# An mLSTM layer whose heads' scores and sums are regrouped on TensorE, with two later issues

## The chip, the cores and the metric

The kernel runs on one core of a Trainium2 chip. Five engines work beside each other: TensorE (PE in the profile; its weight loads are PEld) multiplies matrices into the eight banks of PSUM, VectorE (DVE) and ScalarE (ACT) do elementwise work, GpSimd (POOL) and SyncE (SP) mostly issue transfers here. The metric is the device time of one execution, in microseconds (us). The time before is the median of three runs, 894.86 us (893.63 to 895.79).

## The reference

One decoder layer on 512 tokens of width 1024. A normalised input is multiplied by a wide matrix and feeds two branches: an mLSTM with four heads and a sliding-window attention. Both are merged with sigmoid gates, projected and added to the input; a squared-ReLU MLP and a gated embedding follow, and a last normalisation. The part that matters here, in formulas for one mLSTM head (the kernel takes all 512 tokens as one chunk):

```python
scores = einsum("thk,shk->ts", q, k) * exp(log_d - m_t)   # causal
num = scores @ v ;  den = scores.sum(-1)
h = num / maximum(abs(den), exp(-m_t))
h = h * rsqrt(mean(h * h) + EPS) * norm_g * sigmoid(o)    # y_a
merged = sigmoid(g_a) * (y_a @ w_branch_a) + sigmoid(g_b) * (y_b @ w_branch_b)
x = x + merged @ w_out
...
out = x * rsqrt(mean(x * x) + EPS) * g_fin                # the last norm
```

## The kernel before

All activations stay on the chip; weights stream in as 512 KB transfers on SP's queue. Almost every product has both operands split into a high and a low part (`split`, L133 to L141: ScalarE casts the high part at L137, VectorE subtracts at L138) and is made of three TensorE products (high-high, high-low, low-high) of 512 columns at L171. Weights go through four buffers each of high and low parts (wh, wl), so a weight's cast waits until the product four weights earlier is done with its buffer. The products of the output projection and of the MLP's second half are in a form with seven products of blocks instead of eight, with sums of blocks as operands: `merge_sums` (L887) makes the activations' sums.

PSUM is shared by tags. In the first pool psg has two tiles of one bank, pst two of one bank, psa two of two banks. A tile taken when all are in use waits until one is released. For the output projection the pool is closed and another opened, with three pairs of two banks (psp) and two banks psg at the start of the memory.

The order of the instructions is not the program's. A planner simulates the program and lists, engine by engine, what to issue next among the instructions that it takes to be ready, the earlier in the program first. Each engine then works its list strictly in order, and waits on a semaphore where a real predecessor is late. `tc.keep_in_program_order(ins)` pins an instruction behind the one traced before it on its engine. `with tc.issue_after(ins):` keeps what is traced in the block behind `ins`, but only on the engine of `ins`: instructions of the block that run on another engine are not held.

The mLSTM stage (L767 to L864): `ml_weights(h)` computes a head's decays by ten exponentials on ScalarE (L788), its scores in four products with plain f32 operands into pst banks (L795; each appears as two TensorE instructions), and multiplies both on VectorE (L796). `ml_out(h)` sums the values with these weights, for each of four blocks of 128 tokens in a pst bank (L805, one to four products of 257 columns, the last column being the denominator), copies the result to SBUF on ScalarE (L808) and the denominator on VectorE (L809), and squares it for the norm (L817). `ml_norm` scales the heads (L829), with the output gate fetched back from DRAM. `branch_b(i)` is one of eight products with w_branch_b (24 TensorE products into a psg bank, evicted by VectorE at L838), `ya_of(h)` transposes a head's result (L847). The heads' loop mixes these: two branch products and one head per turn, and the transposes two heads behind.

Then `merge(i)` for i from 0 to 7 multiplies with w_branch_a into psg and evicts at L873 and L874, `merge_sums` follows each second one, and `out_proj` begins: the first product of F11 into X (two psg banks), copied out to q1 by ScalarE (L992) and added to the residual by transfers from GpSimd's queue (L995), then F12 accumulated onto the same X.

At the end of the kernel, `columns_of` (L944) transposes the residual for the last gated product, a psp tile for each column set, evicted by L140 on ScalarE and L141 on VectorE, and `ple` (L1198 evicts) makes the embedding's product. The final gain g_fin is loaded at L1188 and scaled into two versions by L1191 and L1192 on VectorE; it is used in the last norm (L1265, L1281).

`stir` (L259) issues small products into an idle psg tile at the start, to keep TensorE busy.

Of the kernel before, what the change touches and what calls it, by code (L numbers as in the profile page):

```python
# [36 lines left out]
def block_kernel(  # L37
# [221 lines left out]
    idle = ps_g()  # L259

    def stir(n):
        for i in range(n):
            tc.keep_in_program_order(T.matmul(idle[:, :P], ones, ones, start=True, stop=True))
# [8 lines left out]
    for i in range(2):  # L272
        for c in range(2):
            tc.keep_in_program_order(
                T.matmul(gmix[:, c * 512 : (c + 1) * 512], one_row, gparts[c][i], start=i == 0, stop=i == 1, skip_group_check=True)
            )
        stir(1 if i == 0 else 3)
# [495 lines left out]
    def ml_weights(h):  # L773
# [9 lines left out]
        for s in range(NT):  # L783
            dm = act_f("dm")
            n0 = s * P
# [8 lines left out]
            psc = ps_t()  # L794
            T.matmul(psc[:, n0:], qk[4 + h][:, n0 : n0 + P], qk[h][:, n0:], start=True, stop=True)  # L795
            V.tensor_mul(dm[:, n0:], psc[:, n0:], dm[:, n0:])  # L796
            wT.append(dm)
        wts[h] = wT

    def ml_out(h):  # L800
        wT = wts.pop(h)
        for t in range(NT):
            pn = ps_t()
            for s in range(t + 1):
                T.matmul(  # L805
                    pn[:, : DV + 1], wT[s][:, t * P : (t + 1) * P], vm[s][:, h, :], start=s == 0, stop=s == t
                )
            A.copy(h_of(h, t), pn[:, :DV])  # L808
            V.tensor_copy(hd[:, h, t : t + 1], pn[:, DV : DV + 1])  # L809
# [40 lines left out]
    ml_weights(0)  # L850
    rds = []
    for h in range(NH):
        branch_b(2 * h)
        if h + 1 < NH:
            ml_weights(h + 1)
        rds.append(ml_out(h))
        branch_b(2 * h + 1)
        if h == 1:
            ml_norm([0, 1], rds)
        elif h > 1:  # L860
            ml_norm([h], rds[h:])
            ya_of(h - 2)
    ya_of(2)
    ya_of(3)  # L864
# [22 lines left out]
    def merge_sums(even, odd):  # L887
# [8 lines left out]
        for two, src in (((G1, G2), sa), ((G3, G4), sb)):  # L896
            hl = act_hl("ms")
            split(hl, src)
            for n in range(2):
                two[n].append([q[:, n * 256 : (n + 1) * 256] for q in hl])  # L900

# [12 lines left out]
    for j in range(4):  # L914
# [10 lines left out]
        merge_sums(m0, merge(2 * j + 1))  # L925
# [35 lines left out]
    def out_proj():  # L961
# [29 lines left out]
        for t in range(2):  # L991
            A.copy(q1[t], X[t])  # L992
# [198 lines left out]
    V.tensor_scalar_mul(glast, gfin, D**0.5 / 8192)  # L1191
    V.tensor_scalar_mul(gfin, gfin, -(D**0.5) / 8192)  # L1192
# [17 lines left out]
    with tc.issue_after(evicted):  # L1210
        for m in range(NT):
# [181 lines left out]
```

## Time and profile before

| | |
|---|---|
| median of three runs | 894.86 us (893.63 to 895.79) |
| the profiled execution | 894.56 us |
| its span, first to last instruction | 892.8 us |
| granted TensorE clock | 0.999 |
| instructions | 11819 |
| data moved by DMA | 105.19 MB, mean 118 GB/s |

A row of a timeline has the start in us from the span's start, the length in us, the engine, the line of the kernel and the operation, then the tile written and those read ("psg<-ya,wh"), the shapes, and the number of instructions merged into the row. A bracket at its end is the time that the engine stood idle before it, and what ended the wait. TensorE's products overlap in the rows (one starts while the last still drains), so a row's length is more than a product's share of the time. A row by line gives instead the shortest, median and longest duration in ns, the first and last start, and the forms.

### The profile page before, as it was taken

How to read it: one execution, taken by the hardware profiler on the slowest of the kernel's cores; microseconds unless marked ns; L12 is line 12 of the kernel's file. 1: busy time of each engine (PE TensorE's matmuls, PEld its weight loads, DVE VectorE, ACT ScalarE, POOL GpSimd, SP SyncE). 2: the span in 40 equal slices, each digit the busy share in tenths (PEclk: the TensorE clock that was granted, in tenths of full speed). 3: DMA queues.
4: the chain of work that ended last, by engine and by line, in shares of the span. 5: the costliest groups of instructions: out<-in, count | busy, mean ns of one | idle time of the engine just before them, and what ended most of it. 6: DMA issues, size and time to landing. Idle time of an engine off the chain costs nothing.

```text
span 892.8 us, 11819 instructions
## 1 busy us (share of the span) xinstructions
PE 876.9 (98%) x4452; PEld 731.2 (82%) x4452; DVE 665.0 (74%) x1074; ACT 488.6 (55%) x810; POOL 30.3 (3%) x53
## 2 busy tenths in 40 slices
PE   8999999999999999999989999999999999999996
PEld 7888889998877677788878888888888888888786
DVE  6899787874887967557896669746966784699566
ACT  6684554454775767654343566345435534544753
POOL 2111010000000000000020000000000000000000
PEclk9999999999999999999999999999999999999999
DMA  7775254434212162346234711630352054102402
GB/s 273 195 184 177 71 173 162 163 118 165 72 48 72 29 206 74 116 123 240 89 52 136 258 49 39 206 108 25 112 177 88 1 189 142 48 24 61 152 1 95
DMA packets 32363, 105.19 MB, mean 118 GB/s; under 512 B 4525, under 2 KB 5037, under 8 KB 32306
## 3 DMA queue, kind: packets, MB, share of 16 engines
q1 hardware_dynamic: 28002, 93.15, 31.3%
q0 software_dynamic: 4160, 11.02, 4.7%
q8 instruction: 35, 0.57, 0.3%
q10 hardware_dynamic: 144, 0.26, 0.1%
q14 instruction: 22, 0.18, 0.1%
HBM read 91.30 MB, written 8.40 MB: 112 GB/s over the span
## 4 chain that ended last, share of the span: by engine, by line
PE 93%; DMA 2%; DVE 2%; ACT 1%; issue 0%; SPq 0%; DVEq 0%; ACTq 0%
PE psg L171 52%; PE psp L171 23%; PE psa L171 7%; PE pst L171 4%; PE pst L805 2%; PE pst L734 1%; PE psa L726 1%; PE pst L795 1%; PE psa L689 1%; PE psa L690 1%; DMA wr<-in_w_vsif 1%; DMA gfin<-in_g_fin 1%; DMA wr<-in_w_gb 0%; PE pst L847 0%; DVE wl L138 0%
## 5 line engine op out<-in xcount | busy, mean ns | idle before, releaser
L138 DVE TENSOR_TENSOR wl<-wr,wh 128x1024 fp32r<-128x1024 f32 x138 | 167.6, 1220 | 91.7 <-ACT wh L137 91.3
L137 ACT CAST wh<-wr 128x1024 fp32r<-128x1024 f32 x138 | 144.7, 1050 | 163.0 <-PE psg L171 60.8
L171 PE MATMUL psg<-x,wh 128*128 128x512 f32 x512 | 157.7, 389 | 0.0
L171 PE MATMUL psp<-wh,uf 128*128 128x512 f32 x448 | 139.1, 389 | 0.0
L171 PEld LDWEIGHTS psg<-x,wh 128*128 128x128 f32 x512 | 96.0, 188 | 19.9
L171 PE MATMUL psg<-x,wl 128*128 128x512 f32 x256 | 99.6, 389 | 0.0
L171 PEld LDWEIGHTS psp<-wh,uf 128*128 128x128 f32 x448 | 84.1, 188 | 17.3
L171 PE MATMUL psp<-wl,uf 128*128 128x512 f32 x224 | 87.3, 390 | 0.0
L171 PE MATMUL psg<-h,wh 128*128 128x512 f32 x256 | 81.4, 396 | 0.0
L137 ACT CAST wh<-wd 128x1024 fp32r<-128x1024 f32 x44 | 46.3, 1053 | 57.1 <-PE psp L171 23.1
L138 DVE TENSOR_TENSOR wl<-wd,wh 128x1024 fp32r<-128x1024 f32 x44 | 53.3, 1220 | 15.5 <-ACT wh L137 15.4
L171 PEld LDWEIGHTS psg<-h,wh 128*128 128x128 f32 x256 | 46.9, 188 | 13.5 <-issue 4.9
L171 PEld LDWEIGHTS psg<-x,wl 128*128 128x128 f32 x256 | 48.1, 188 | 9.9
L171 PE MATMUL psg<-h,wl 128*128 128x512 f32 x128 | 50.3, 393 | 0.0
L138 DVE TENSOR_TENSOR uf<-F,uf 128x1792 fp32r<-128x1792 f32 (+2 forms) x20 | 33.0, 1652 | 22.1 <-ACT uf L137 22.1
L171 PEld LDWEIGHTS psp<-wl,uf 128*128 128x128 f32 x224 | 42.1, 188 | 8.7
L171 PE MATMUL psg<-yb,wh 128*128 128x512 f32 x128 | 43.2, 411 | 0.0
L171 PE MATMUL psg<-ya,wh 128*128 128x512 f32 x128 | 40.1, 393 | 0.0
L137 ACT CAST uf<-F 128x1792 fp32r<-128x1792 f32 (+2 forms) x20 | 27.9, 1395 | 20.8 <-DVE F L1095 20.7
L1119 DVE SCALAR_TENSOR_TENSOR xk<-psp,r,xk 128x512 f32<-128x512 f32 x48 | 33.9, 746 | 3.5 <-PE psp L171 3.2
L171 PE MATMUL psg<-hS,wh 128*128 128x256 f32 x192 | 35.6, 284 | 0.0
L171 PE MATMUL psa<-h,wh 128*128 128x256 f32 x192 | 35.3, 285 | 0.3 <-ACT p L625 0.3
(313 smaller groups left out, 1782.3 us busy)
## 6 DMA issues: line engine op xcount, KB each, us to landing
wr<-in_w_up SPq DMA_DIRECT2D x32, 512.0 KB, 3.3
wd<-in_w_down SPq DMA_DIRECT2D x24, 512.0 KB, 3.7
wr<-in_w_qsw SPq DMA_DIRECT2D x8, 512.0 KB, 4.1
gd<-gr POOLq DMA_DIRECT2D x8, 512.0 KB, 3.3
wr<-in_w_qkml SPq DMA_DIRECT2D x8, 512.0 KB, 3.4
wr<-in_w_b SPq DMA_DIRECT2D x8, 512.0 KB, 3.3
gl<-gd SPq DMA_DIRECT2D x8, 512.0 KB, 3.3
wr<-in_w_a SPq DMA_DIRECT2D x8, 512.0 KB, 3.8
```

The lines of the kernel that those rows point to most:

```text
L137: A.copy(dst[0], src)
L138: last_low[0] = V.tensor_sub(dst[1], src, r32(dst[0]))
L171: last_mm[0] = T.matmul(ps, l, r, start=first and i == 0, stop=last and i == len(ops) - 1, skip_group_check=parts)
L689: T.matmul(o, q[:, n * P : (n + 1) * P], kk[kp][ab][:, k0 : k0 + 256], start=True, stop=False)
L690: T.matmul(o, q[:, n * P : (n + 1) * P], kl[kp][ab][:, k0 : k0 + 256], start=False, stop=True)
L726: T.transpose(pt[:, c : c + P], lm3[ab][:, g, j * P : (j + 1) * P], ident)
L734: T.matmul(o[HALF[ab], :], vs[n + 1 - nk + j][:, c : c + 64], pTs[j][:, ab * 512 : (ab + 1) * 512], start=j == 0, stop=j == nk - 1,)
L795: T.matmul(psc[:, n0:], qk[4 + h][:, n0 : n0 + P], qk[h][:, n0:], start=True, stop=True)
L805: T.matmul(pn[:, : DV + 1], wT[s][:, t * P : (t + 1) * P], vm[s][:, h, :], start=s == 0, stop=s == t)
L1119: pin(V.scalar_tensor_tensor(o, ps[:, t, :], r2[:, 2 * toks + t : 2 * toks + t + 1], o, ALU.mult, ALU.add))
```

## The change

Four things change. (1) A head's decays (`ml_decay`) are separated from its scores (`ml_scores`). The scores go into one psa tile of two banks and one pst bank, the score for s=3 sharing a bank with that for s=1; the sums go two token blocks at a time into the two banks of a psa tile and are evicted together, the later half first. A head's sums are kept behind its branch product, and the next head's scores behind these sums. One branch product is left in each turn of the loop; the other four come after it, each followed by the transposes of one head. (2) The idle tile at the start becomes two. (3) The second half of the last `merge_sums` is returned as a function and called after the copies to q1. (4) The two scalings of g_fin move into the block after the last copy of the embedding's product.

```diff
-    idle = ps_g()
+    idle = [ps_g(), ps_g()]
-    def stir(n):
+    def stir(n, bank=0):
         for i in range(n):
-            tc.keep_in_program_order(T.matmul(idle[:, :P], ones, ones, start=True, stop=True))
+            tc.keep_in_program_order(T.matmul(idle[bank][:, :P], ones, ones, start=True, stop=True))
...
-        stir(1 if i == 0 else 3)
+        stir(1 if i == 0 else 3, i)
...
-    def ml_weights(h):
+    def ml_decay(h):
...
-            psc = ps_t()
-            T.matmul(psc[:, n0:], qk[4 + h][:, n0 : n0 + P], qk[h][:, n0:], start=True, stop=True)
-            V.tensor_mul(dm[:, n0:], psc[:, n0:], dm[:, n0:])
...
+    def ml_scores(h):
+        two, one = ps_a(), ps_t()
+        banks = [two[:, :512], two[:, 512:], one, two[:, 512:]]
+        at = [0, 0, 0, 384]
+        for s in (0, 1, 3, 2):
+            n0 = s * P
+            psc = banks[s][:, at[s] : at[s] + S - n0]
+            T.matmul(psc, qk[4 + h][:, n0 : n0 + P], qk[h][:, n0:], start=True, stop=True, skip_group_check=True)
+        for s in range(NT):
+            n0 = s * P
+            dm = wts[h][s]
+            V.tensor_mul(dm[:, n0:], banks[s][:, at[s] : at[s] + S - n0], dm[:, n0:])
...
     def ml_out(h):
         wT = wts.pop(h)
-        for t in range(NT):
-            pn = ps_t()
-            for s in range(t + 1):
-                T.matmul(
-                    pn[:, : DV + 1], wT[s][:, t * P : (t + 1) * P], vm[s][:, h, :], start=s == 0, stop=s == t
-                )
-            A.copy(h_of(h, t), pn[:, :DV])
-            V.tensor_copy(hd[:, h, t : t + 1], pn[:, DV : DV + 1])
+        for half in (1, 0):
+            pn = ps_a().rearrange("p (n c) -> p n c", n=2)
+            for t in (2 * half, 2 * half + 1):
+                for s in range(t + 1):
+                    last_mm[0] = T.matmul(
+                        pn[:, t % 2, : DV + 1], wT[s][:, t * P : (t + 1) * P], vm[s][:, h, :], start=s == 0, stop=s == t, skip_group_check=True
+                    )
+            A.copy(hs[h][half].rearrange("p (n c) -> p n c", n=2), pn[:, :, :DV])
+            V.tensor_copy(hd[:, h, 2 * half : 2 * half + 2], pn[:, :, DV])
...
-    ml_weights(0)
+    ml_decay(0)
+    ml_scores(0)
     rds = []
     for h in range(NH):
-        branch_b(2 * h)
+        branch_b(h)
         if h + 1 < NH:
-            ml_weights(h + 1)
-        rds.append(ml_out(h))
-        branch_b(2 * h + 1)
+            ml_decay(h + 1)
+        with tc.issue_after(last_mm[0].ins):
+            rds.append(ml_out(h))
+        if h + 1 < NH:
+            with tc.issue_after(last_mm[0].ins):
+                ml_scores(h + 1)
         if h == 1:
             ml_norm([0, 1], rds)
         elif h > 1:
             ml_norm([h], rds[h:])
-            ya_of(h - 2)
-    ya_of(2)
-    ya_of(3)
+    for h in range(NH):
+        branch_b(NH + h)
+        ya_of(h)
...
-        for two, src in (((G1, G2), sa), ((G3, G4), sb)):
+
+        def parts(two, src):
             hl = act_hl("ms")
             split(hl, src)
...
+        parts((G1, G2), sa)
+        return lambda: parts((G3, G4), sb)
...
-        merge_sums(m0, merge(2 * j + 1))
+        later = merge_sums(m0, merge(2 * j + 1))
+        if j < 3:
+            later()
...
-            A.copy(q1[t], X[t])
+            copied = A.copy(q1[t], X[t])
+        with tc.issue_after(copied.ins):
+            later()
...
-    V.tensor_scalar_mul(glast, gfin, D**0.5 / 8192)
-    V.tensor_scalar_mul(gfin, gfin, -(D**0.5) / 8192)
...
     with tc.issue_after(evicted):
+        V.tensor_scalar_mul(glast, gfin, D**0.5 / 8192)
+        V.tensor_scalar_mul(gfin, gfin, -(D**0.5) / 8192)
```

More of the change, by code (lines that the diff above doesn't have):

```diff
@@ L784, in ml_weights @@
             dm = act_f("dm")
-            n0 = s * P
             for t in range(s, NT):
```

## The prediction

> **What bounds the kernel now.** I read the page's busy table first, then a table of stretches, then the chain of waits, then the timelines of TensorE (PE), ScalarE (ACT) and VectorE (DVE) around each place that the diff touches.
>
> ```profile
> PE 876.9 (98%) x4452; PEld 731.2 (82%) x4452; DVE 665.0 (74%) x1074; ACT 488.6 (55%) x810; POOL 30.3 (3%) x53
> PE 93%; DMA 2%; DVE 2%; ACT 1%; issue 0%; SPq 0%; DVEq 0%; ACTq 0%
> 338.80:414.00 75.20, 75.20 (x336) 58.86 (x336) 44.58 (x101) 47.52 (x115) 0.00 (x0) 1.00 0.41 139
> 452.40:461.10 8.70, 6.21 (x26) 4.88 (x27) 8.66 (x14) 5.95 (x9) 0.01 (x1) 1.00 0.00 0
> 824.80:840.80 16.00, 14.60 (x80) 11.99 (x79) 10.69 (x15) 10.64 (x17) 0.00 (x0) 1.00 0.58 195
> ```
>
> TensorE is busy for 98% of the span and makes up 93% of the chain that ended last. A change can therefore shorten the kernel only where TensorE stands still or loses time between products. The three stretches are the ones that the diff touches; after the length and a comma, their columns are busy time and count of PE, PEld, DVE, ACT and POOL, then TensorE's granted clock. In the mLSTM stretch (338.8 to 414) TensorE is covered for all 75.20 us, so nothing like an idle gap can be won there. At the start of the output projection (452.4 to 461.1) it stands still for 2.5 us of 8.7, and at the last norm's columns for 1.4 us of 16. The clock is full in all three.
>
> ```profile
> 443.40 0.61 PE L171 MATMUL psg<-ya,wh 128*128 128x512 f32 x2
> 443.85 0.39 PE L171 MATMUL psg<-ya,wl 128*128 128x512 f32 x1
> 444.08 0.61 PE L171 MATMUL psg<-ya,wh 128*128 128x512 f32 x2
> 453.27 0.47 PE L171 MATMUL psg<-wh,mg 128*128 128x512 f32 x1 [0.88 <-DVE sga L873]
> 460.60 0.50 PE L171 MATMUL psg<-wh,mg 128*128 128x512 f32 x1 [1.62 <-ACT q L992]
> 824.81 1.04 PE L944 MATMUL psp<-ident,xk 128*128 128x128 f32 x8
> 831.66 0.60 PE L944 MATMUL psp<-ident,xk 128*128 128x128 f32 x4
> 833.05 0.66 PE L944 MATMUL psp<-ident,xk 128*128 128x128 f32 x4 [0.79 <-DVE x L141]
> 834.31 0.66 PE L944 MATMUL psp<-ident,xk 128*128 128x128 f32 x4 [0.61 <-DVE x L141]
> ```
>
> The first three rows give the pitch: three products of 512 columns between 443.40 and 444.08, so 0.227 us each, though a row alone shows 0.39. The brackets in the other rows are the stalls and what ended them. They are the raw material of this prediction.
>
> **The change part by part.**
>
> *The bank at the start of the output projection.* Products with w_a take the two banks of psg in turn. With one idle tile, the idle tile and the uses up to merge(7) make 49 (1 idle, 4 for vs, 8 q, 8 qk, 12 as Z, 8 branch_b, 8 merge), so merge(7) has the first bank, which X[0] of the new pool takes too. The 453.27 row agrees: the first product of the projection waited for the multiplication at L873.
>
> ```profile
> 449.65 0.68 DVE L873 TENSOR_TENSOR sga<-psg,gl 128x512 f32<-128x512 f32 x1
> 452.44 0.69 DVE L873 TENSOR_TENSOR sga<-psg,gl 128x512 f32<-128x512 f32 x1 [0.37 <-PE psg L171]
> 453.05 0.42 DVE L138 TENSOR_TENSOR mg<-sga,mg 128x256 fp32r<-128x256 f32 x1
> ```
>
> The second row reads merge(7)'s bank until 453.13, the first read merge(6)'s until 450.33. TensorE's last merge product ended at 452.39 (453.27 less 0.88), the next ended at 453.74 where 452.62 was due: 1.12 us lost. With two idle tiles there are 50 uses, so X[0] falls on merge(6)'s bank, free for 2 us, and X[1], first needed six products (1.36 us) later, on a bank that is free by then. Bounds: nothing, if slots are not taken in strict turn, to 1.1 us. I take **-1.0**. What is late next are the casts of F11, but the last of them (third row) ends at 453.5 and the half that needs it starts at 455.1 (12 products after 452.39).
>
> *The casts of the last sums.* Before the first part of the product can be copied out (q1, L992), ScalarE does this:
>
> ```profile
> 456.35 1.06 ACT L137 CAST wh<-wr 128x1024 fp32r<-128x1024 f32 x1 [1.58 <-PE psg L171]
> 457.31 0.62 ACT L137 CAST ms<-ms 128x512 fp32r<-128x512 f32 x1
> 458.37 0.62 ACT L137 CAST ms<-ms 128x512 fp32r<-128x512 f32 x1 [0.43 <-DVE ms L895]
> 459.02 1.04 ACT L137 CAST wh<-wr 128x1024 fp32r<-128x1024 f32 x1
> 459.97 1.07 ACT L992 COPY q<-psg 128x512 f32<-128x512 f32 x2
> ```
>
> TensorE ended the first product's 24 multiplications at 458.98 (460.60 less 1.62). X[0] had been complete since six multiplications before that, at 457.6, yet its copy started at 459.97, behind the second sums' cast (0.62) and a weight cast (1.04). The change puts the second sums' cast behind the copies, and its product comes 48 multiplications (11 us) later, which covers it. If the copy of X[0] then starts when X[0] is complete, TensorE doesn't stop: 1.62 idle and 0.27 of slow restart (460.60 + 0.50 against a pitch of 0.227) are won, 1.9 us. If the weight cast stays ahead of the copies, next to nothing is won, since that cast itself starts when the 24 multiplications end. I take **-1.6**, nearer to the first: with one entry fewer ScalarE is free when X[0] completes, and the weight cast isn't yet.
>
> *The last norm's scalings.* VectorE's queue:
>
> ```profile
> 827.69 1.23 DVE L138 TENSOR_TENSOR wl<-wr,wh 128x1024 fp32r<-128x1024 f32 x1
> 831.64 0.69 DVE L1191 TENSOR_SCALAR glast<-gfin 128x1024 f32<-128x1024 f32 x1 [2.73 <-DMA gfin<-in_g_fin]
> 832.25 0.74 DVE L141 SCALAR_TENSOR_TENSOR x<-psp,gple,x 128x512 fp32r<-128x512 f32 x1
> 832.91 0.68 DVE L1192 TENSOR_SCALAR gfin<-gfin 128x1024 f32<-128x1024 f32 x1
> 828.02 1.29 ACT L140 ACTIVATE x<-psp,gple 128x512 fp32r<-128x512 f32 x2
> 843.57 1.23 DVE L138 TENSOR_TENSOR wl<-wr,wh 128x1024 fp32r<-128x1024 f32 x1 [5.01 <-ACT wh L137]
> L1281 DVE TENSOR_TENSOR z<-xk,gfin x3: 684/684/685, 863.1 to 867.3; 128x512 f32<-128x512 f32 x3
> ```
>
> VectorE stood 2.73 us at the scaling, waiting for the transfer of gfin, with two column sets behind it that ScalarE had finished by 829.3. Their psp tiles stayed taken, and the transposes waited. The four-transpose set ending at 833.71 took 1.45 us after the one ending at 832.26, the next 1.26; without a wait a set adds 0.44 (eight transposes at 824.81 take 1.04, four take 0.60). That is 1.0 + 0.8 = 1.8 us. Traced after the second projection, the two scalings (1.4 us) have the 5.01 us gap ahead of 843.57 to lie in, and nothing reads gfin before 863. Bounds: 0 to -1.8; I take **-1.6**.
>
> *The mLSTM heads.* The products stay the same in number and shape; their order, their banks and their evictions change.
>
> ```profile
> L805 PEld LDWEIGHTS pst<-vm,dm x80: 186/190/190, 350.9 to 401.3; 128*128 128x128 f32 x80
> 386.58 0.39 PE L171 MATMUL psg<-yb,wh 128*128 128x512 f32 x1
> 386.85 3.30 PE L805 MATMUL pst<-vm,dm 128*128 128x257 f32 x14
> 386.85 2.87 PE L805 MATMUL pst<-vm,dm 128*128 128x257 f32 x12
> 339.00 1.65 PE pst L795 x4
> 413.38 0.44 PE pst L847 x4
> ```
>
> Two more instructions add 0.43 us (3.30 against 2.87), so 0.215 each. The run of 14 should take 3.02; from the end of the product ahead (386.97) to its own end (390.15) it takes 3.18, so entering it cost 0.16. The chain of waits has 23 separate pieces of scores, sums and transposes between 338.8 and 414, of which the last two rows are the first and the last. After the change there are about nine: the first scores, four runs of a head's sums with the next head's scores, and four groups of transposes. Fourteen entries go. One costs between nothing and 0.16 where I can read it; 0.1 gives -1.4.
>
> The Trainium skill ("TensorE: Matmul & The Clock Gate", section on LDWEIGHTS) gives a weight load as columns over 1.2, an estimate of 0.107 us for 128 columns; if each entry bared one load, 14 would be 1.5 us. This trace's loads take longer (186 to 190 ns in the L805 row), which would make 2.6.
>
> Against it stand new waits. A head's sums now fill an attention tile of two banks before it is evicted, and the next head's scores need the first of these tiles back.
>
> ```profile
> 351.66 0.37 ACT L808 COPY hs<-pst 128x256 f32<-128x256 f32 x1 [1.82 <-PE pst L805]
> 352.06 0.16 DVE L809 COPY hd<-pst 128x1 f32<-128x1 f32 x1 [0.94 <-ACT hs L808]
> L1198 ACT COPY pe<-psg x8: 585/587/612, 827.5 to 841.0; 128x512 f32<-128x512 f32 x8
> wr<-in_w_b SPq DMA_DIRECT2D x8, 512.0 KB, 3.3
> ```
>
> The copy of the denominators follows ScalarE's copy of the same tile. One eviction is thus 0.59 (the L1198 copy has the new size) + 0.16 and some 0.15 of passing on: 0.9 us. The other half's six instructions cover 6 x 0.215 = 1.3 us of it, so the scores don't wait if ScalarE and VectorE come at once. Either may be busy: with a weight cast (1.04) on ScalarE just begun, 0.6 us shows, and with VectorE's counterpart (1.23) as well, 1.8. I allow 0.3 at each of three heads, +0.9. The branch products that used to stand between heads move behind the last head; each of heads 1 to 3 still has 24 of them (5.4 us) over its decay weights, and 18 of merge(0)'s (4.1 us) cover the last transposes' casts. The queues that the branch products are moved past: on SP the loads of w_b and of the gates keep their order among themselves, and only the og loads of heads 2 and 3 change places with those of the last four; such a load lands in 3.3 us, and the DMA engines are 41% busy in this stretch, so I cost this at nothing. POOL only gets the accumulations of q1, as early as q1 is. Net **-0.5**, bounds -1.4 and +4.5.
>
> **Sum.** What is won at 452 must last to the end:
>
> ```profile
> 461.10:824.80 363.70, 363.70 (x1625) 301.41 (x1625) 266.73 (x309) 179.12 (x208) 5.28 (x6) 1.00 0.33 105
> ```
>
> Between the two places TensorE is covered throughout, with DMA at 33%, so nothing there waits for a clock time rather than for TensorE's own progress. -1.0 - 1.6 - 1.6 - 0.5 = -4.7. The profiled execution took 894.56 (span 892.8 and 1.76 around it), 0.3 under the median of 894.86. This gives 889.9 against the one and 890.2 against the other; I forecast **890.0**.
>
> **The rivals.**
>
> *A planned order doesn't move as intended.* The instruction order is made ahead by a planner that issues, per engine, what it takes to be ready. The block around the scalings holds back only the queue of the instruction it names, the copy at L1198 on ScalarE; the scalings run on VectorE, so only their later place in the program speaks for a move. VectorE may seem idle to the planner just there, and the 2.73 us wait remains: 891.6 (1.6 over the forecast). Likewise the weight cast may stay ahead of q1: also 891.6. For it: that cast already stands ahead of copies that are earlier in the program. Against it: two column sets and X[0] were ready when each queue chose. Both at once: 893.2, within what counts as no change.
>
> *Eviction stalls, the slower side.* If an eviction takes longer than the 1.3 us that the half-run covers, all of TensorE waits, since the scores are queued right behind the sums. At 1.8 us for each of three heads (both casts in the way) it is +5.4 in place of +0.9, which takes back all the rest: 894.5 with the gains, 897.7 with both of the others missing as well. It is slower than before as soon as the three waits total 5.6 with the gains, or 2.4 without the planner's two. Speaking for it: in this stretch TensorE never idles, because branch products could slip into any hole; the change takes some of these away. Against it: ACT and DVE are busy 47.5 and 44.6 of 75.2 us, and the planner can still put the next branch product in front.
>
> The Trainium skill ("PSUM — Partial Sum Buffer", section on bank collisions) has it that no two engines may use one bank at once, reads against reads included. By it the scores for s=1 and s=3, now in one bank, could be read only when both are written; nothing in this trace shows that pairing.
>
> **How the numbers follow.** All four parts as summed: 0.42 (890.0, itself 888.8 to 890.9). One planned order not moving: 0.26 (891.6). Both, or half of the eviction stalls: 0.16 (893.2 to 895). Eviction stalls that decide: 0.16 (897). A measurement of this kernel tells about 0.2% (1.8 us) from no change, so faster is below 893.1: 0.67 with small remainders, same 0.17, slower 0.16. The range goes from 888.8, all bounds of the stalls, to 895.5, leaving out most of the last case.
>
> **What would show it.** The 0.88 us wait at the first projection product gone and its releaser no longer L873; L992's first copy starting ahead of a weight cast, with no stall of TensorE behind it; L1191 standing behind the column sets, with no DMA wait ahead of an L141; sums and the next head's scores in three runs of 28 instructions (20 and 8) and one of 20, and no bracket in them that names L808 or L809. Wrong would be: a new PE stall on psa in the mLSTM stretch, or TensorE's gaps closed and the span no shorter.

## The result, and the profile after

The changed kernel takes 889.65 us (median of 6 runs, 888.75 to 890.39) against 894.84 for the kernel before in the same session (893.63 to 895.79, 6 runs): a ratio of 0.9942, 95% interval 0.9929 to 0.9954. The forecast was 890.0 with a range of 888.8 to 895.5. The profiled execution took 889.58, with a span of 887.8 (892.8 before).

The busy table of the changed kernel's page, and a table of stretches that answer to the three of the prediction (length and a comma, then busy time and count of PE, PEld, DVE, ACT and POOL, granted clock, DMA share, GB/s):

```profile
PE 875.5 (99%) x4452; PEld 733.5 (83%) x4452; DVE 663.1 (75%) x1066; ACT 486.8 (55%) x802; POOL 30.3 (3%) x53
```

```profile
338.80:412.70 73.90, 73.74 (x338) 59.76 (x337) 46.25 (x96) 46.95 (x107) 0.00 (x0) 1.00 0.41 143
451.10:459.00 7.90, 7.69 (x35) 6.03 (x34) 7.82 (x13) 5.92 (x9) 1.71 (x4) 1.00 0.04 7
821.50:836.00 14.50, 14.45 (x80) 12.05 (x79) 10.71 (x15) 10.44 (x18) 0.00 (x0) 1.00 0.61 210
```

TensorE stands still for 0.21 us at the start of the output projection (2.5 before) and for 0.05 at the last norm's columns (1.4 before). In the mLSTM stretch it now has 0.16 of idle time that it didn't have, and the stretch is shorter all the same: what went there does not show as idle time in TensorE's rows.

TensorE at the first projection products of the changed kernel, then ScalarE beside it:

```profile
450.75 0.39 PE L171 MATMUL psg<-ya,wl 128*128 128x512 f32 x1
450.98 0.39 PE L171 MATMUL psg<-wh,mg 128*128 128x512 f32 x1
456.79 0.50 PE L171 MATMUL psg<-wh,mg 128*128 128x512 f32 x1 [0.21 <-ACT q L1013]
```

```profile
455.63 0.62 ACT L137 CAST ms<-ms 128x512 fp32r<-128x512 f32 x1 [0.62 <-DVE ms L908]
456.16 1.10 ACT L1013 COPY q<-psg 128x512 f32<-128x512 f32 x2
457.15 0.62 ACT L137 CAST ms<-ms 128x512 fp32r<-128x512 f32 x1
457.67 1.05 ACT L137 CAST wh<-wr 128x1024 fp32r<-128x1024 f32 x1
```

The first projection product follows the last merge product at the pitch (0.23), with no bracket. The copies (L992 before, L1013 now) stand ahead of the second sums' cast and of the weight cast. They still stand behind the first sums' cast, which itself waited 0.62 us for VectorE, so 0.21 of the 1.62 us wait is left.

VectorE at the last norm's columns of the changed kernel:

```profile
825.47 1.40 DVE L141 SCALAR_TENSOR_TENSOR x<-psp,gple,x 128x512 fp32r<-128x512 f32 x2
827.60 0.69 DVE L1232 TENSOR_SCALAR glast<-gfin 128x1024 f32<-128x1024 f32 x1 [0.73 <-DMA gfin<-in_g_fin]
829.68 2.07 DVE L141 SCALAR_TENSOR_TENSOR x<-psp,gple,x 128x512 fp32r<-128x512 f32 x3 [0.66 <-ACT x L140]
```

The scalings did not go to the far gap where the forecast put them. The planner put both two column sets later, into a hole in which no column set was ready; the next set after them waited for ScalarE, not for a transfer.

The heads' scores (L804) and sums (L816) on TensorE in the changed kernel; the branch products between them are left out:

```profile
354.93 4.50 PE L816 MATMUL psa<-vm,dm 128*128 128x257 f32 x20
359.58 1.99 PE L804 MATMUL psa<-acc,acc 128*128 128x512 f32 x6 [0.16 <-DVE hd L820]
361.41 0.60 PE L804 MATMUL pst<-acc,acc 128*128 128x256 f32 x2
...
365.75 4.50 PE L816 MATMUL psa<-vm,dm 128*128 128x257 f32 x20
370.08 0.59 PE L804 MATMUL pst<-acc,acc 128*128 128x256 f32 x2
...
374.64 1.89 PE L804 MATMUL psa<-acc,acc 128*128 128x512 f32 x6
```

A head's twenty instructions of sums stand in one piece (the first head's, at 346, are still cut by branch products). Only once do the scores follow the sums in one run, at 359.58, and that is the one place where they wait for the eviction. At 370.08 the planner put branch products between the scores of the free bank and those that need the evicted tile.

**Where the time went, by stretches of TensorE.** Each stretch runs from the end of one instruction to the end of another, the same in all kernels: the end of the first norm's last transposes, the first TensorE product of the first branch product (reads yb), the last merge product (ya), the last product that reads mg, the last down product (uf), the last that reads pT, the last of all.

| stretch to the end of | before | after | difference |
|---|---|---|---|
| first-norm transposes | 21.92 | 22.40 | +0.48 |
| first branch product | 311.64 | 311.60 | -0.04 |
| last merge product (mLSTM heads, merge) | 118.84 | 117.14 | -1.70 |
| last product with mg (output projection) | 35.69 | 33.15 | -2.54 |
| last down product | 336.88 | 337.33 | +0.45 |
| last product with pT (last norm's columns) | 15.95 | 14.34 | -1.61 |
| last product | 45.01 | 45.02 | +0.01 |

The differences add up to -4.95. The total came out as forecast, but not by the forecast's own terms: the heads gave 1.2 more, and two losses of 0.5 each, where the prediction saw nothing happen, took most of that back. That it came out so close is in part luck.

### The profile page after: what moved, and what is told of

The parts are those of the page before. It is cut to its first block, busy times and chain, and to the rows that moved or that the text cites. A ratio compares the mean times of both kernels' runs of the same rounds, so it can differ in the third digit from the quotient of the medians.

```text
span 887.8 us, 11800 instructions
## 1 busy us (share of the span) xinstructions
PE 875.5 (99%) x4452; PEld 733.5 (83%) x4452; DVE 663.1 (75%) x1066; ACT 486.8 (55%) x802; POOL 30.3 (3%) x53
## 4 chain that ended last, share of the span: by engine, by line
PE 93%; DVE 3%; ACT 2%; DMA 1%; issue 1%; SPq 0%; ACTq 0%; DVEq 0%
PE psg L171 52%; PE psp L171 22%; PE psa L171 7%; PE pst L171 4%; PE pst L734 1%; PE psa L816 1%; PE psa L726 1%; PE psa L689 1%; PE psa L690 1%; DVE wl L138 1%; PE psa L804 1%; PE psg L263 1%; DMA wr<-in_w_gb 0%; PE pst L858 0%; PE psp L973 0%
## 5 line engine op out<-in xcount | busy, mean ns | idle before, releaser
L171 PEld LDWEIGHTS psg<-h,wh 128*128 128x128 f32 x256 | 46.9, 188 | 13.5 <-issue 4.9
```

The costliest lines, as they stand in the source:

```text
L171: last_mm[0] = T.matmul(ps, l, r, start=first and i == 0, stop=last and i == len(ops) - 1, skip_group_check=parts)
```

## The experiments

The theory to test: four places, each with a wait of its own, whose gains add. The rivals: the parts need each other, the heads' gain is one of order and not of banks, and the losses belong to the change. Where nothing is changed the stretches above repeat to 0.3 us, but for three: the start (21.73 to 23.76), the one after it (311.53 to 312.25 over all kernels) and the last norm's columns in the old form. So each experiment is read in the stretch that its edit touches; times stand beside it.

**Each part alone, on the kernel before.** The four edits are the hunks of the diff, each by itself. Eleven or twelve runs of each are compared with 35 of the kernel before (median 895.33).

The second idle tile:

```diff
-    idle = ps_g()
+    idle = [ps_g(), ps_g()]
```

> The kernel before with only the second idle tile. Theory (the first bank of psg was still being read by L873's multiplication of merge(7)): the 0.88 us wait at the first projection product goes, the time falls by 1.0 us and nothing else changes. Rival A (the casts of F11 or the weight cast are late next): another releaser takes the bracket and less than 0.3 us is won. Rival B (the second idle tile is what slowed the start, where the changed kernel's first-norm transposes end 0.47 us later than in the kernel before): the start is 0.4 to 0.5 us longer here too, and 0.5 us is won in all.

Measured: 896.63 us, ratio 1.0016 (1.0007 to 1.0026), so slower. The profile splits this. The projection's stretch is 35.56 (35.69 before): the wait at its first product is gone, and nothing is won. The start took 23.62 in the profiled execution against 21.92, and that is where this execution lost. The kernel with the scalings alone, with one idle tile, has 23.55 there, so a late start doesn't need the second tile. Why most runs of this one kernel are late stays open. TensorE in this kernel, then ScalarE:

```profile
454.34 0.39 PE L171 MATMUL psg<-wh,mg 128*128 128x512 f32 x1
462.57 0.50 PE L171 MATMUL psg<-wh,mg 128*128 128x512 f32 x1 [2.63 <-ACT q L992]
```

```profile
460.47 0.62 ACT L137 CAST ms<-ms 128x512 fp32r<-128x512 f32 x1 [0.85 <-DVE ms L895]
461.00 1.04 ACT L137 CAST wh<-wr 128x1024 fp32r<-128x1024 f32 x1
461.94 1.06 ACT L992 COPY q<-psg 128x512 f32<-128x512 f32 x2
```

TensorE starts the projection 1.1 us sooner and then waits 2.63 for the copy in place of 1.62. The copy stands behind the second sums' cast, and that waits for VectorE's sums, which don't come sooner because TensorE does. Rival A had the size (under 0.3) but not the place: almost all of the time won at one wait was handed over to a later one.

The second sums' cast later:

```diff
-        merge_sums(m0, merge(2 * j + 1))
+        later = merge_sums(m0, merge(2 * j + 1))
+        if j < 3:
+            later()
```

> The kernel before with only the second sums' cast put behind the q1 copies. Theory (ScalarE's queue, not TensorE's products, set when X[0] was copied): the 1.62 us wait shrinks to about 0.2, the time falls by 1.4 to 1.6 us, and the weight cast stands behind the copies. Rival (the weight cast keeps its place ahead of the copies unless the first bank's wait is also gone): the copy starts 0.4 us earlier at most, and less than 0.5 us is won.

Measured: 893.43, ratio 0.998 (0.9971 to 0.9988); the stretch is 33.77, 1.92 shorter. ScalarE in this kernel:

```profile
458.68 0.61 ACT L137 CAST ms<-ms 128x512 fp32r<-128x512 f32 x1
459.19 0.57 ACT L998 COPY q<-psg 128x512 f32<-128x512 f32 x1
460.44 0.59 ACT L998 COPY q<-psg 128x512 f32<-128x512 f32 x1 [0.67 <-PE psg L171]
...
461.44 1.05 ACT L137 CAST wh<-wr 128x1024 fp32r<-128x1024 f32 x1
```

The second copy now waits for TensorE, and not the reverse; no stall for the copies is left (the 0.88 at the first product stands). The weight cast moved behind the copies by itself. The theory holds; the size is the upper bound of the prediction's term, above the 1.4 to 1.6 expected here.

The scalings later:

```diff
     with tc.issue_after(evicted):
+        V.tensor_scalar_mul(glast, gfin, D**0.5 / 8192)
+        V.tensor_scalar_mul(gfin, gfin, -(D**0.5) / 8192)
```

> The kernel before with only the two scalings traced later. Theory (VectorE stood at the first scaling for the transfer of gfin, with two column sets behind it): the scaling's wait no longer has column sets behind it, the two waits of TensorE there (0.79 and 0.61 us) go, and the time falls by 1.6 us. Rival (TensorE waits there for the column sets' own chain of ScalarE and VectorE): one of the waits stays, and at most 0.8 us is won.

Measured: 894.18, ratio 0.9989 (0.998 to 0.9997). The stretch is 14.58 against 15.95 (1.37 of the 1.6 expected), and both waits of TensorE that named VectorE's column sets are gone. But the two kernels above, which keep the scalings' old place, have 15.48 and 14.91 in the same stretch. VectorE's wait for gfin was 2.29 and 1.69 us there, against 2.73: how much the old place costs hangs on when that transfer lands.

The heads:

> The kernel before with only the mLSTM part (new banks, runs, pins, and the branch products at the end). From the two traces, the mLSTM and merge stretch is 1.70 us shorter, so theory: 1.7 us is won here, all of it between 338 and 452. Rival A (the forecast's net of 0.5): 0.5 us, with waits of the scores of about 0.3 us at each of three heads. Rival B (the stretch is only shorter because the other parts moved the planner's order): under 0.3 us.

Measured: 893.80, ratio 0.9985 (0.9974 to 0.9995). The mLSTM stretch is 117.14, just as in the changed kernel; 1.70 is this part's own. The twelve runs spread from 891.32 to 896.32, and the profiled one is the fastest: it had an early start (21.73) and a short wait for gfin (1.48).

**The bank, with everything else in place.**

```diff
-    idle = [ps_g(), ps_g()]
+    idle = [ps_g()] * 2
```

> The changed kernel with one idle tile in place of two, so that X[0] falls on merge(7)'s bank again. The stretch from the last merge product to the last product with mg took 35.69 in the kernel before, 35.56 with the second idle tile alone, 33.77 with the later sums alone, 33.15 in the changed kernel. Theory (the bank is worth 0.62 us once ScalarE's queue no longer sets the next stall, and 0.13 while it does): 33.77, with the 0.88 us wait back, and no change of the start that goes beyond its own scatter (21.7 to 23.6 so far). Rival (the bank is worth its 1.1 us here): 34.25.

Measured: 33.76 (theory 33.77); 891.10, ratio 0.9954 (0.9941 to 0.9968). So the bank is worth 0.61 us beside the later cast and 0.13 without it, and the cast 1.92 without the bank and 2.41 (35.56 less 33.15) with it.

**The old place of the scalings, on another engine.**

```diff
-    V.tensor_scalar_mul(glast, gfin, D**0.5 / 8192)
-    V.tensor_scalar_mul(gfin, gfin, -(D**0.5) / 8192)
+    G.tensor_scalar_mul(glast, gfin, D**0.5 / 8192)
+    G.tensor_scalar_mul(gfin, gfin, -(D**0.5) / 8192)
```

> The kernel before with the two scalings at their old place but on GpSimd, which has nothing else to do there. The stretch from the last down product to the last product with pT took 15.95 and 16.16 in two executions of the kernel before, 15.48, 14.91 and 14.71 in three kernels that keep the old place but waited less for gfin, and 14.34 to 14.58 with the later place. Theory (column sets stood behind VectorE's wait for the transfer of gfin): 14.3 to 14.6 here too, however late gfin lands. Rival (the later place gave VectorE's 1.4 us of scalings room, and the wait itself did no harm, or the column sets are late for a reason of their own): 15 or more.

Measured: 14.36, and 893.62 us in its one run. GpSimd and TensorE in this kernel:

```profile
831.10 2.79 POOL L1191 TENSOR_SCALAR glast<-gfin 128x1024 f32<-128x1024 f32 x1 [364.12 <-PE psg L171]
```

```profile
832.26 1.47 PE L944 MATMUL psp<-ident,xk 128*128 128x128 f32 x12
```

The first scaling starts at 831.10 and takes four times as long as on VectorE, and TensorE's transposes no longer wait (twelve of them run on from 832.26). That VectorE's column sets stood behind its wait for gfin is thereby shown.

**The heads, order and banks apart.** First the new order alone, with the old single banks:

```diff
     for h in range(NH):
-        branch_b(2 * h)
+        branch_b(h)
         if h + 1 < NH:
             ml_weights(h + 1)
         rds.append(ml_out(h))
-        branch_b(2 * h + 1)
...
+    for h in range(NH):
+        branch_b(NH + h)
+        ya_of(h)
```

> The kernel before with only the order of the mLSTM part changed: branch products 4 to 7 and all transposes for the merge behind the last head; scores, sums and evictions as before, in single banks. From the end of the first branch product to the end of the last merge product the kernel before takes 118.84 us, the changed one 117.14. Theory (most of it is entries into sums, read as 0.95 us of excess over the pitch, and this order only saves the wait of the first merge products for the last transposes' casts, 0.43 us of excess): 118.4. Rival (the order is all of it): 117.2.

Then the changed kernel with the branch products and transposes back in the old order, and the attention's banks kept:

```diff
-        branch_b(h)
+        branch_b(2 * h)
...
+        branch_b(2 * h + 1)
         if h == 1:
             ml_norm([0, 1], rds)
         elif h > 1:
             ml_norm([h], rds[h:])
-    for h in range(NH):
-        branch_b(NH + h)
-        ya_of(h)
+            ya_of(h - 2)
+    ya_of(2)
+    ya_of(3)
```

> The changed kernel with the branch products and transposes back at their old places between the heads; the heads' sums and scores stay in the attention's banks with their pins. Same stretch (before 118.84, changed 117.14). Theory (the runs and banks give what the order doesn't): 117.6. Rival A (without the branch products' new order, the scores wait for evictions at each head): over 119. Rival B (the order is all of it): 118.8.

| mLSTM stretch, us | old banks | attention's banks |
|---|---|---|
| old order | 118.84 to 119.11 (six executions) | 119.24 |
| new order | 120.22 | 117.11 to 117.22 (six executions, the longest with the eviction doubled) |

Both forecasts missed: 118.4 and 117.6 were expected. The second run's rival A ("over 119") has the size, but its reason, evictions at each head, is not what the trace shows. Alone, the order costs 1.1 to 1.4 and the banks gain nothing; together they gain 1.7 or more. (Times: the order alone on the kernel before, 896.57, ratio 1.0015, 1.0006 to 1.0025. The changed kernel with the old order, 891.97, ratio 0.9958, 0.9941 to 0.9975.) The traces show what stands in the way of each. Each TensorE product's row ends some time after the one ahead; what that is more than the usual pitch of its form, added up over the stretch, gives the time lost:

| us beyond the pitch | before | banks alone | order alone | changed |
|---|---|---|---|---|
| scores and sums of the heads | 1.6 | 0.4 | 3.6 | 0.6 |
| transposes, branch and merge products | 0.8 | 2.4 | 0.2 | 0.1 |
| both | 2.4 | 2.8 | 3.8 | 0.7 |

The banks take the loss out of the heads and the order takes it out of the merge, but each alone adds more on the other side. TensorE in the kernel with the new order and single banks:

```profile
380.25 5.19 PE L805 MATMUL pst<-vm,dm 128*128 128x257 f32 x22 [0.55 <-DVE dm L796]
```

With half of the branch products moved away, scores and sums in two single banks wait for VectorE (here 0.55 us). In the kernel with the attention's banks and the old order, the sums run through as in the changed one, and the loss comes later, at the merge. TensorE, then VectorE:

```profile
415.07 0.50 PE L171 MATMUL psg<-ya,wh 128*128 128x512 f32 x1 [1.16 <-DVE ya L141]
```

```profile
413.12 1.23 DVE L941 TENSOR_TENSOR wo<-wo,wo 128x1024 f32<-128x1024 f32 x1 [1.56 <-DMA wo<-in_w_out]
414.26 1.41 DVE L141 SCALAR_TENSOR_TENSOR ya<-pst,gml,ya 128x512 fp32r<-128x512 f32 x2
```

The last transposes' casts stand behind L941, which waited 1.56 us for the load of w_out. It is the same trap as at gfin: a VectorE instruction that waits for a transfer, with casts behind it that TensorE needs. In the new order, branch products lie between the last transposes and the merge, and the casts are done in time.

**The eviction doubled.** In the changed kernel, ScalarE copies each half of the sums out twice:

```diff
+            for _ in range(2):
-            A.copy(hs[h][half].rearrange("p (n c) -> p n c", n=2), pn[:, :, :DV])
+                A.copy(hs[h][half].rearrange("p (n c) -> p n c", n=2), pn[:, :, :DV])
```

> The changed kernel with each head's sums copied out twice by ScalarE (eight copies of 0.57 us more, same result). It prices the eviction: in the changed kernel scores waited for it at one place only (0.42 us over the pitch, with 0.16 of idle, at 359.58). Theory (branch products fill the other places): the same place grows by about 0.6, the stretch is 117.7 in place of 117.14. Rival (each of the three heads stands at the edge): 3 x 0.6, 118.9.

Measured: 117.22, 0.08 more (891.06 us in its one run); neither the 0.6 nor the 1.8. The second head's sums, then the scores of the third and the fourth, in this kernel on TensorE:

```profile
357.36 4.50 PE L816 MATMUL psa<-vm,dm 128*128 128x257 f32 x20
361.70 0.59 PE L804 MATMUL pst<-acc,acc 128*128 128x256 f32 x2
362.13 1.96 PE L804 MATMUL psa<-acc,acc 128*128 128x512 f32 x6
373.77 0.39 PE L171 MATMUL psg<-yb,wl 128*128 128x512 f32 x1
374.24 1.96 PE L804 MATMUL psa<-acc,acc 128*128 128x512 f32 x6
```

The planner now takes the free bank's scores first, so those that need the evicted tile start 0.27 us after the sums' end (361.86) in place of 0.15, and without a bracket. The place that had cost 0.42 costs 0.08 here. But at 374.24, the third such place, the six instructions end 2.04 after the product ahead (376.20 against 374.16) where 1.73 is due: 0.3 that the changed kernel doesn't lose there. The wait moved to another head, and the longer eviction added almost nothing to the sum.

**The kernel before once more.**

> The kernel before, unchanged: another execution of it, to see what varies by itself. Theory: its start (end of the first-norm transposes, 21.92 in the profile shown) lies anywhere in 21.7 to 23.6, and the stretch from the last down product to the last product with pT (15.95 in the profile shown, with a wait of 2.73 us for the transfer of gfin) in 14.7 to 16.0, with the wait; all other stretches repeat to 0.2. Rival (start and gfin's landing belong to each kernel): 21.9 and 15.9 again.

Measured: 895.90; the start 22.80 (21.92 in the profile shown), the last norm's columns 16.16 (15.95), the mLSTM stretch 119.11 (118.84), all other stretches the same to 0.02. Start and wait for gfin therefore vary by themselves, as the theory had it, though the last norm's columns went a little over its 16.0 and the mLSTM stretch over its 0.2. Over the twelve executions that have no more than the usual idle products the start lies between 21.73 and 23.76, with either number of idle tiles (one: 21.73 to 23.76 in eight; two: 22.28 to 23.62 in four). TensorE at the start, in the kernel before and in the one with only the scalings moved, which issues the same there:

```profile
12.07 0.40 PE L171 MATMUL psg<-wh,h 128*128 128x264 f32 x2
12.31 0.28 PE L171 MATMUL psg<-wl,h 128*128 128x264 f32 x1
```

```profile
11.75 0.59 PE L171 MATMUL psg<-wl,h 128*128 128x264 f32 x1 [1.42 <-DVE wl L328]
12.14 0.64 PE L171 MATMUL psg<-wh,h 128*128 128x264 f32 x2
12.58 0.42 PE L171 MATMUL psg<-wl,h 128*128 128x264 f32 x1
...
17.78 0.41 PE L171 MATMUL psg<-wh,h 128*128 128x264 f32 x2
```

Two products take 0.24 from one row's start to the next in the first kernel (12.07 to 12.31) and 0.44 in the second (12.14 to 12.58), so a pitch of 0.12 and of 0.22. In the second the pitch is 0.12 only from 17.8, with the same instructions: until then its products run at half rate.

**No wait at the start.** The changed kernel with three idle products behind the first transposes:

```diff
     on_scalar, _ = columns(0, xn)
+    stir(3, 1)
```

> The changed kernel with three idle products (six instructions of about 0.21 us) behind the first transposes, where TensorE otherwise waits 1.0 to 1.5 us for the first low weights. The first-norm transposes ended between 21.73 and 23.62 in ten executions, and the later ends had products of 264 columns at 0.22 us in place of 0.12 after that wait. Theory (the wait lets TensorE's rate fall, for a time that differs from run to run): the start ends at 21.8 or less, the median falls by 0.5 to 1 us against the changed kernel's. Rival (the rate at the start follows something other than this wait): the end lies in the same scatter, or up to 0.5 us later as the idle products run into the first product's place.

Measured: the start ends at 21.46, sooner than in all twelve others; 889.27 us, ratio 0.9936 (0.9924 to 0.9949). The five runs lie within 0.28 us of each other (889.25 to 889.53), where the changed kernel's six lie within 1.64. Against the changed kernel's 0.9942 the intervals overlap, so the median is not shown to be lower. The start is earlier in both kernels with the idle products (this one and the next), one execution of each; that the runs are steadier is not shown, since the next kernel's five spread over 1.00 us. The theory's reason, that the wait lets the rate fall, fits two of the twelve other executions: in seven the rate rose only after the wait, and in three it stayed up (last section). TensorE here:

```profile
9.65 1.49 PE L263 MATMUL psg<-ones 128*128 128x128 f32 x6
```

**And p loaded sooner.** The same with the first block of p in a tile of its own, loaded ahead of the up and down products:

```diff
-            t = ep.tile([P, PLE], F32, tag="ptok", bufs=4, name=nm("ptok"))
-            nc.sync.dma_start(out=t, in_=p[m * P : (m + 1) * P, :])
+            t = p0
+            if m:
+                t = ep.tile([P, PLE], F32, tag="ptok", bufs=4, name=nm("ptok"))
+                nc.sync.dma_start(out=t, in_=p[m * P : (m + 1) * P, :])
...
+    p0 = cp.tile([P, PLE], F32, name="p0")
+    nc.sync.dma_start(out=p0, in_=p[:P, :])
```

> The same with the first block of p loaded well ahead, which takes the wait for p (0.20 to 0.45 us of idle, 0.42 to 0.8 with the restart, in the three kernels that hold all four parts) away from the transposes of p: the stretch from the last product with mg to the last down product 336.9 in place of 337.33. Theory: 0.4 us less than with the idle products alone, the fastest of all kernels here, 888.4 to 889.2. Rival (the second block of p lands late as well): 337.3 again.

Measured: 888.60 us (888.29 to 889.29), ratio 0.9928 (0.9916 to 0.9941), the lowest of all kernels here; the start 21.46 again, the stretch to the last down product 337.03 (336.9 expected), and no wait for p. Against the changed kernel its median is 1.05 us lower, but the two intervals against the kernel before overlap; what the traces show is a start 0.94 and a down stretch 0.30 shorter.

## Why the prediction was right, and where it wasn't

*The bank at the start of the output projection, -1.0.* The wait was what the prediction said, and it went. But as a term by itself it was wrong: 0.13 alone, 0.61 beside the later cast. The step that failed is "what is late next", which looked at the casts of F11 and not at the copies for q1: those followed VectorE's sums, not TensorE, and took nearly the whole gain.

*The casts of the last sums, -1.6.* Right in mechanism and in the weight cast's place. 1.92 alone, and with the bank 2.54 against a forecast of 2.6 for both: the pair fits because one term was too large by about as much as the other was too small. The bound named (the copy of X[0] at its completion) was not reached in the changed kernel: X[0] was complete six products before 456.58, at 455.2, and the copy starts at 456.16, behind the first sums' cast.

*The last norm's scalings, -1.6.* 1.61 against the execution that the sum was made against. Six executions with the old place on VectorE took 14.71 to 16.16 in this stretch (mean 15.55; the sixth, 16.08, is the kernel with the new order alone), so against their mean it is 1.2. The mechanism is shown by GpSimd's run. The prediction's place for the scalings was wrong: they went into a nearer hole and keep a wait of 0.73 for the transfer, which nothing stands behind.

*The heads, -0.5.* Measured -1.70. This term was off in size at both its ends, and one end also in mechanism. "0.3 at each of three heads" for evictions came out as 0.42 at one and nothing at the others. At 359.58 the six instructions of the scores end at 361.57, 2.14 after the sums' end; on the chain of waits of the changed kernel the six that follow branch products take 1.73:

```profile
374.81 1.73 PE psa L804 x6
```

The others cost nothing because the planner puts branch products there, as the prediction held possible and priced at nothing.

The gain was priced at 0.1 for each entry into a run, fourteen fewer (eleven came out: 12 runs are left of 23). But an entry by itself costs nothing. On the chain of the changed kernel, the first head's sums are still cut in three by branch products, and the third head's stand in one piece:

```profile
346.53 0.43 PE psa L816 x2
347.42 0.43 PE psa L816 x2
348.31 3.47 PE psa L816 x16
365.91 4.33 PE psa L816 x20
```

Three pieces take 0.43 + 0.43 + 3.47 = 4.33, as much as one. In the kernel before, the twenty take more even in one piece, and the weight loads (PEld) show why, where TensorE's own overlapping rows have no bracket:

```profile
350.95 4.63 PE pst L805 x20
386.85 0.73 PEld L805 LDWEIGHTS pst<-vm,dm 128*128 128x128 f32 x4 [0.31 <-DVE hd L809]
408.08 0.53 PEld L171 LDWEIGHTS psg<-ya,wh 128*128 128x128 f32 x3 [0.42 <-ACT ya L140]
```

The second row is the entry from which the prediction read 0.16: its weight load waited for the copy of a denominator out of a single pst bank (L809). Most of the costly entries are of this kind. Of the 2.4 us lost beyond the pitch before the change, 1.3 lie at nine places where a weight load waited for L809 or L796 to be done with a pst bank or the decay weights, and 0.27 at 408.08, where it waited for the last transposes' casts. None of these ten waits is left in the changed kernel, which loses 0.7, 0.42 of it at the one eviction. So what went were short waits for single banks and casts, not a cost of switching; the step that failed is the price per entry, read from one such wait. That order and banks are worth nothing or less singly the prediction, adding entries and waits, could not give.

*What it left out.* The start's +0.48 lies within what the kernel before does by itself, so it says nothing of the change. The +0.45 before the last down product is a wait for p, with the restart after it. SP issues its loads in the same order in both kernels. SP's transfers of p in the kernel before, then in the changed one, with TensorE behind them:

```profile
791.99 1.75 SPq L1166 DMA_DIRECT2D ptok<-in_p  x4
```

```profile
788.19 1.94 SPq L1189 DMA_DIRECT2D ptok<-in_p  x4
791.16 0.44 PE L1192 MATMUL psg<-ident,ptok 128*128 128x128 f32 x2 [0.20 <-DMA ptok<-in_p]
```

The wait stands in five kernels (the changed one, those with the eviction doubled, the old order, one idle tile, and the idle products: 0.14 to 0.47) and in none of the eight that hold at most one of the four parts. The first load is issued 2.1 to 2.2 us ahead of the first transposes in all of them. It is the second block that is late: in the five, SP issues its load 0.66 us after the first (788.85 after 788.19 in the changed kernel), in the eight 0.38 or 0.39, and it lands 2.2 to 2.6 us after its issue against 2.1. Each of the five, and none of the eight, has an 8 KB load of instructions in this stretch, 0.65 to 0.90 us after that issue. Whether this load, or what called for it, holds SP up is not shown. Loading one block sooner removes the wait.

*The rivals.* The planner's order did move at both places. The eviction stalls that would have made the kernel slower are 0.42 in all, far from the 5.6 at which they decide. The Trainium skill's rule on bank collisions ("PSUM — Partial Sum Buffer") was not put to a test of its own; in the changed kernel's rows VectorE starts to read the third head's psa tile at 361.61, after the last score in it ended at 361.57, which agrees with it but shows no cause. The list of signs was right for the projection and partly for the scalings; it was wrong for the heads, where one bracket names the copy of the denominators (L809 before, L820 now) and the scores join the sums only once in a run.

## What to carry to other kernels

A wait that ends sooner on the bounding engine is a gain only if the next thing it needs comes from its own progress: follow the chain to the next wait, and ask which engine sets that one. Where two edits share a cover (here the branch products between heads), price them as a pair, since each alone can lose what both win. A stall of less than the overlap of TensorE's rows has no bracket there: look at the weight loads' rows before calling it a fixed cost. An instruction that waits for a transfer is dear by what stands behind it in its queue; look for those first, because their cost also moves with the landing, and one profile shows only one landing.

## What the runs showed of the hardware

At the start, the same instructions ran at two rates: products of 264 columns at a pitch of 0.12 or of 0.22 us. In all executions TensorE runs at half rate from its first products at 1.05 us until its wait of 1.0 to 1.5 us for the first low weights (or the idle products in its place), though it is busy for all of the 8.8 us from 1.1 to 9.9. What differs is when the trace's record of the granted clock rises to 1.00, and the end of the start follows it:

| clock rises at, us | end of the start | executions |
|---|---|---|
| 10.1 to 10.7 | 21.73 to 21.92 | 3 |
| 10.1, half again from 13.5 to 16.9 | 22.80 to 22.82 | 2 |
| 14.8 to 15.6 | 22.28 to 22.73 | 4 |
| 17.7 to 18.0 | 23.55 to 23.76 | 3 |
| 11.3 and 12.3, with the idle products in the wait | 21.46 | 2 |

The two executions of the kernel before stand in the first and the second row. So in two of twelve the rate fell after the wait, and in seven it rose only later. A view of the granted clock can mislead here. First the kernel with only the scalings moved, then the second execution of the kernel before (only TensorE's columns are asked for):

```profile
14.80:16.80 2.00, 2.00 (x11) 1.00 0.87 311
```

```profile
14.80:16.80 2.00, 2.00 (x10) 0.50 0.77 236
```

Both stretches are at half rate (10 or 11 instructions in 2 us), and only one of them shows 0.50: in the other execution the trace's first clock record begins at 17.73, and the column shows 1.00 where there is none. The pitch must be read beside it; it turns to 0.12 at 17.78 there.

The Trainium skill ("TensorE: Matmul & The Clock Gate", part 1) has it that TensorE's clock is halved until it has been busy through a window of some 3.4 us, and that these windows run freely, so that one kernel starts differently from run to run. The traces agree in part: the rate is one half or full, nothing between; in the two executions of the second row the record falls and rises again at steps of 3.41 us; and the rise comes at other times in other executions of one kernel. But 8.8 busy us, more than two such windows, pass in all fourteen before the earliest rise at 10.1, and why they did not raise the clock is not shown. That the idle products bring an early rise by filling the wait fits both executions that have them; two are few against free-running windows.
